# Loads of the first latent head and of the convolutions' gates, issued from ScalarE's queue instead of SyncE's

## The chip, the cores and the metric

One core of a Trainium2 chip runs the whole program in one launch. The metric is device time in microseconds (us), from repeated runs of the same program; the median counts. The engines are TensorE (PE, matrix products; PEld is its loading of weights), VectorE (DVE), ScalarE (ACT), GpSimd (POOL) and SyncE (SP). SP does no arithmetic here: it issues transfers between the chip's large memory (HBM) and the on-chip memory. ACT can issue transfers too. An engine takes its instructions strictly in order, a transfer's issue among them: an instruction that waits holds up all that stand behind it on that engine.

## What is computed

Two layers of a trunk over 1152 tokens (1024 latent, 128 context), width 1024, all in 32-bit floating point. Each layer mixes tokens in four groups of heads that share one input projection, and then applies an MLP:

```python
mq, ckv, kpe, sq, sk, sv, gqkv, gz, ga, gb, hu = project(h, P['w_in'])
o_a = dense_attention(q_a, k, v, MLA_QK ** -0.5, None)     # 4 latent-attention heads
o_b = banded_attention(q_b, k_b, v_b, k_c, v_c, P['swa_sink'])
o_c, _, _ = gdn_mixer(gqkv, gz, ga, gb, P, st[:, 0], st[:, 1])   # delta-net scan
o_d = hyena_mixer(hu, P)                                   # long convolutions
...
z = x1 * long_conv_centred(v, filt[0], P['hy_bias'][0])    # inside hyena_mixer
return x2 * long_conv_centred(z, filt[1], P['hy_bias'][1])
...
x = x + gt1 * rms_norm(merge_heads(o_a, o_b, o_c, o_d), P['g_post_mix'])
x = x + gt2 * rms_norm(square(relu(h @ mlp_w1)) @ mlp_w2, P['g_post_mlp'])
```

The factors x1 and x2 are the gating values of the convolutions. Each layer also needs a modulation vector, a product of the conditioning vector with a weight `w_ada` of 1024 x 6144.

## The kernel before, in words

The program is one long list of instructions made by Python generators; a planner (`TileContext(nc, schedule_with_timeline_sim=True)`) decides at compile time, by its own simulated times, in which order each engine gets them and which buffer each tile takes, and adds the waits. Two generators may therefore end up interleaved on an engine, but what is written first has precedence.

Per layer the input projection runs first and parks its results in HBM (`kscr`, `krscr`, `qscr`, `qrscr`, `vascr` for the latent heads, `uscr` for the three parts v, x1, x2 of the convolutions, `gscr`, `sscr`, `suscr`, `goscr` for the scan). Then three things run side by side, started by `run_timed` at the end of the first half of `layer`: the convolutions (`hyena`, two calls of `long_conv`) followed by attention; the delta-net scan (`gdn_scan`, with precedence by `high_priority`); and the modulation products (`ada`), which stream 256 KB pieces of `w_ada` (tiles `wada`, four buffers in tag T, more in L for the very first) through PE.

`hyena` loads v, the transform matrices and small things, and calls `long_conv` for o = 0 and o = 1. After each it loads x1 or x2 in two halves of 128 x 1024 numbers (512 KB each) with `load(1 + o, i, "x")` and multiplies on DVE (line 1734). The first latent head's `mla_prep` is started from inside the second convolution through `ahead`: its first step issues 16 loads, for Q and K (each a main and a rest part, put together from pieces of 64, 32 and 1 rows), V and one more tile E, and the steps after that compute the scores S on PE and their row maxima on DVE (line 772). Then the negated maxima go by way of HBM (`mscr`) into row 96 of Q, and `mla_main` computes the transposed scores (tile ST), their exponentials on ACT and the weighted sums.

Q, K and V of heads 0, 1 and 3 and all work tiles of the convolutions come from the same pool of 12 buffers (`self.big`), so a load of head 0 has to wait until the convolution is done with a buffer. Head 2 uses the scan's pool.

In the scan each step has a chain of small operations: products on PE (tiles u, dS), an addition on DVE (line 1370), the state's decay on ACT (line 1357), scaled copies on ACT (line 1388) with additions on DVE (line 1389), and stores into `goscr` issued by SP (line 1392). Loads of `wada` are line 392, loads of x and v line 1706, those of head 0 lines 752 to 760. Every transfer of the kernel before is issued by SP.

Of the kernel before, what the change touches and what calls it, by code (L numbers as in the profile page):

```python
# [10 lines left out]
F32 = mybir.dt.float32  # L11
# [9 lines left out]
T = 1152  # L21
# [142 lines left out]
class Trunk:  # L164
# [576 lines left out]
    def mla_prep(self, l, h):  # L741

        nc = self.nc
        tag = self.gdn_tag if h == 2 else self.big
        Q = [self.W(dt=F32R, name="Q", tag=tag) for _ in range(2)]
        K = [self.W(dt=F32R, name="K", tag=tag) for _ in range(2)]
        V = self.W((9, 128), F32R, name="VA", tag=tag)
        E = self.H((128,), F32R, name="vE")
        hp, hr = h // 2, slice(64 * (h % 2), 64 * (h % 2) + 64)
        for i in range(2):  # L750
            for dst, n, r in ((slice(0, 64), self.kscr[l, hp, i], hr), (slice(64, 96), self.krscr[l, i], slice(0, 32))):
                nc.sync.dma_start(out=K[i][dst].bitcast(F32), in_=n[r, 0:T])
                nc.sync.dma_start(out=Q[i][dst, 1024:T].bitcast(F32), in_=n[r, T:1280])
            nc.sync.dma_start(out=Q[i][:64, 0:1024].bitcast(F32), in_=self.qscr[l, hp, i, hr, 0:1024])
            nc.sync.dma_start(out=Q[i][64:96, 0:1024].bitcast(F32), in_=self.qrscr[l, i, 32 * h:32 * h + 32, 0:1024])
            if i == 0:
                nc.sync.dma_start(out=K[0][96:97].bitcast(F32), in_=self.krow[:, 0:T])
                nc.sync.dma_start(out=Q[0][96:97, 1024:T].bitcast(F32), in_=self.krow[:, 0:128])
        nc.sync.dma_start(out=V.bitcast(F32), in_=self.vascr[l, h, 0:9].rearrange("m p c -> p m c"))
        nc.sync.dma_start(out=E.bitcast(F32), in_=self.vascr[l, h, 9])  # L760
        self.job[h] = (Q, K, V, E)
        mx = self.S((8, 3), "mx", 2)
        yield
        for t in range(8):
            q = Q[0][:96, t * 128:t * 128 + 128]
            for a in range(3):
                n = 384 if a < 2 else 512
                ps = self.P(name="S", tag="S" if h else "P")
                self.mm(ps[:, :384], q, K[0][:96, 384 * a:384 * a + 384])
                if a == 2:  # L770
                    self.mm(ps[:, 384:], q, Q[0][:96, 1024:T])
                nc.vector.tensor_reduce(out=mx[:, t, a:a + 1], in_=ps[:, :n], axis=AX.X, op=ALU.max)
                yield
        yield
        yield
        m = self.S((8,), "nm", 2, F32R)
        self.neg_max(m, mx)
        self.row_out(l, h, m.bitcast(F32), 8)
        self.row = nc.sync.dma_start(out=Q[0][96:97, 0:1024].bitcast(F32), in_=self.mscr[l, h:h + 1, 0:1024])
        yield  # L780
# [919 lines left out]
    def hyena(self, l, oT, ahead):  # L1700

        nc = self.nc

        def load(g, i, name):
            t = self.W((4, 256), name=name, tag=self.big)
            nc.sync.dma_start(out=t, in_=self.uscr[l, g, 4 * i:4 * i + 4].rearrange("m p c -> p m c"))
            return t
        fwd = self.dft_mats("fwd", self.small)
        cur = [load(0, i, "v") for i in range(2)]
        inv = self.dft_mats("inv", self.other)  # L1710
        hp = self.W((2, 512), name="hp", tag=self.big)
        for r in (slice(0, 96), slice(96, 97)):
            nc.sync.dma_start(out=hp[r], in_=self.hpscr[l, r])
        up = self.W((3, 256), name="up", tag=self.big)
        nc.sync.dma_start(out=up, in_=self.uscr[l, :, 8].rearrange("g p c -> p g c"))
        up = [up[:, g] for g in range(3)]
        z = up[0]
        fi = self.H(name="fwdp")
        fwdp, invp = (fi[:, a:b].rearrange("p (c f) -> p c f", c=2) for a, b in ((0, 194), (194, 450)))
        nc.sync.dma_start(out=fwdp, in_=self.I["fwdp"])  # L1720
        nc.sync.dma_start(out=invp, in_=self.I["invp"])
        yield HY
        for o in range(2):
            conv = self.long_conv(l, o, cur, fwd, inv, ahead)
            for i, t in enumerate(conv):
                if i == 1:
                    po = self.prompt_conv(l, o, z, hp, fwdp, invp)
                    z = self.H((256,), name="pz")
                    nc.vector.tensor_tensor(out=z, in0=po, in1=up[1 + o], op=ALU.mult)
                yield t  # L1730
            y = self.res
            for i in range(2):
                x = load(1 + o, i, "x")
                nc.vector.tensor_tensor(out=y[i], in0=y[i], in1=x, op=ALU.mult)
            cur = y
        for _ in range(24):
            ahead()
        for c in range(2):
            q = slice(128 * c, 128 * c + 128)
            for m0, src in ((0, cur[0]), (4, cur[1]), (8, z.unsqueeze(1))):  # L1740
                mn = 4 if m0 < 8 else 1
                pt = self.P((4, 128), name="hoT", tag="P")
                for j in range(mn):
                    self.tr(pt[:, j], src[:, j, q])
                oT(6 + c, pt[:, :mn].rearrange("p m t -> p (m t)"), slice(m0 * 128, (m0 + mn) * 128))
            yield HY
# [502 lines left out]
```

## Time and profile before

| | |
|---|---|
| median of 3 runs | 3819.6 us (3818.95 to 3856.05) |
| the profiled execution | 3818.92 us |
| its span, first to last instruction | 3817.1 us |
| PE busy | 3530.3 us, 92% of the span |
| weight loads of PE | 2940.8 us, 77% |
| DVE busy | 2236.0 us, 59% |
| ACT busy | 1367.0 us, 36% |
| POOL busy | 710.1 us, 19% |
| mean granted clock of TensorE | 0.952 of full speed |
| data moved by all transfers | 405.40 MB, mean 106 GB/s |

The busy times are those of one profiled execution and of the whole span; PE's weight loads overlap its products. Issuing a transfer does not count as busy time. Busy shares of the whole span say little about a single stretch, so the rows below are taken from the stretches in which the moved loads are issued.

### The profile page before, as it was taken

Reading aid. Unit: us, or ns where it says so; the run is one execution under the profiler, and the core shown is the slowest. Engines: PE = TensorE matmul, PEld = TensorE weight load, DVE = VectorE, ACT = ScalarE, POOL = GpSimd, SP = SyncE. Lnnn points to the kernel's source line nnn. Section 1 sums busy time; section 2 is a strip of 40 time slices with the busy share of each in tenths; the row PEclk is TensorE's granted clock in tenths of the full one; section 3 lists DMA queues with packets and bytes.
Section 4 is the critical chain, followed back from the end, with each engine's and each line's share of the span. In section 5 each row is a group of like instructions: output and inputs, shape, how many; then the busy total and the mean of one; then the engine's idle time right before and its main releaser. Section 6 shows DMA issues by size and latency. Waiting matters only on the chain. (4 is left out here: it accounts for less than half of the span.)

```text
span 3817.1 us, 58820 instructions
## 1 busy us (share of the span) xinstructions
PE 3530.3 (92%) x22478; PEld 2940.8 (77%) x22478; DVE 2236.0 (59%) x4583; ACT 1367.0 (36%) x2972; POOL 710.1 (19%) x710
## 2 busy tenths in 40 slices
PE   7989888799899999999989798787989999999998
PEld 4879774366689999999968787545656899999997
DVE  5765567677645444444586674767774544444446
ACT  5434343265543122212364334323664422222112
POOL 1152531013420000000131633211143200000003
PEclk9998889799999999999999898897989999999999
DMA  5346476832421111111334465755414211111113
GB/s 203 115 115 158 137 266 201 240 84 60 141 86 48 42 45 44 35 44 45 100 104 129 112 151 151 262 185 167 101 40 138 72 45 45 45 45 45 39 39 122
DMA packets 364677, 405.40 MB, mean 106 GB/s; under 512 B 115816, under 2 KB 237158, under 8 KB 364395
## 3 DMA queue, kind: packets, MB, share of 16 engines
q1 hardware_dynamic: 364394, 401.63, 35.1%
q8 instruction: 177, 2.90, 0.3%
q14 instruction: 106, 0.86, 0.1%
HBM read 298.34 MB, written 103.19 MB: 105 GB/s over the span
## 5 line engine op out<-in xcount | busy, mean ns | idle before, releaser
L213 PE MATMUL hid<-hT,w1h 128*128 128x384 f32 x3072 | 786.6, 335 | 0.1
L213 PE MATMUL pj<-hT,wah 128*128 128x384 f32 x2112 | 575.8, 351 | 10.4 <-ACT wah L253 4.2
L1839 DVE TENSOR_TENSOR acc<-acc,mo 128x512 f32<-128x512 f32 x504 | 345.9, 686 | 391.9 <-PE mo L213 391.9
L213 PEld LDWEIGHTS hid<-hT,w1h 128*128 128x128 f32 x3072 | 557.6, 188 | 14.4 <-ACT h L481 1.1
L213 PE MATMUL hid<-hT,w1l 128*128 128x384 f32 x1536 | 514.1, 335 | 0.0
L213 PE MATMUL mo<-w2h,ul 128*128 128x512 f32 x1116 | 435.0, 392 | 0.0
L213 PE MATMUL mo<-w2h,uh 128*128 128x512 f32 x1080 | 422.7, 391 | 0.0
L213 PE MATMUL mo<-w2l,uh 128*128 128x512 f32 x1080 | 422.7, 391 | 0.0
L213 PEld LDWEIGHTS pj<-hT,wah 128*128 128x128 f32 x2112 | 396.3, 196 | 23.3 <-issue 7.5
L213 PE MATMUL pj<-hT,wal 128*128 128x384 f32 x1056 | 368.2, 349 | 0.7 <-DVE wal L232 0.7
L242 ACT CAST w2h<-w 128x512 fp32r<-128x512 f32 x128 | 70.3, 619 | 732.7 <-PE mo L213 728.5
L269 POOL TENSOR_TENSOR postr<-postr,mhalf 128x1 f32<-128x1 f32 x36 | 22.3, 622 | 1564.1 <-DVE postr L268 1563.7
L213 PEld LDWEIGHTS hid<-hT,w1l 128*128 128x128 f32 x1536 | 288.3, 188 | 2.5
L213 PEld LDWEIGHTS mo<-w2h,ul 128*128 128x128 f32 x1116 | 209.6, 188 | 46.1
L662 POOL TENSOR_TENSOR e<-e,e 128x512 f32<-128x512 f32 (+1 forms) x120 | 162.2, 1353 | 445.3 <-ACT e L651 267.4
L213 PEld LDWEIGHTS mo<-w2h,uh 128*128 128x128 f32 x1080 | 202.8, 188 | 37.5
L213 PEld LDWEIGHTS mo<-w2l,uh 128*128 128x128 f32 x1080 | 202.7, 188 | 36.5
L232 DVE TENSOR_TENSOR el<-e,eh 128x512 fp32r<-128x512 f32 (+1 forms) x252 | 202.3, 820 | 32.2 <-ACT eh L653 30.3
L213 PEld LDWEIGHTS pj<-hT,wal 128*128 128x128 f32 x1056 | 206.4, 195 | 4.6 <-issue 2.0
L1822 DVE SCALAR_TENSOR_TENSOR relu<-hid,relu 128x384 f32<-128x384 f32 x180 | 99.4, 553 | 167.2 <-ACT relu L1821 167.2
L213 PE MATMUL ada<-wada,cst 128*32 128x512 f32 x384 | 137.0, 688 | 46.9 <-DMA wada<-in_w_ada 46.7
L1821 ACT ACTIVATE relu<-hid 128x384 f32<-128x384 f32 x180 | 87.8, 488 | 184.8 <-PE hid L213 184.8
(502 smaller groups left out, 6318.1 us busy)
## 6 DMA issues: line engine op xcount, KB each, us to landing
w<-in_w SPq DMA_DIRECT2D x256, 256.0 KB
wada<-in_w_ada SPq DMA_DIRECT2D x192, 256.0 KB
wa<-in_wa SPq DMA_DIRECT2D x88, 256.0 KB
x<-xres SPq DMA_DIRECT2D x21, 512.0 KB
x<-in_x SPq DMA_DIRECT2D x18, 512.0 KB
Q<-rscr SPq DMA_DIRECT2D x32, 288.0 KB
o<-oscr SPq DMA_DIRECT2D x18, 512.0 KB
xres<-x SPq DMA_DIRECT2D x36, 256.0 KB
```

The source lines that it names most:

```text
L213: self.last = self.nc.tensor.matmul(out, l, r, start=start, stop=stop, skip_group_check=True)
L232: self.nc.vector.tensor_tensor(out=lo, in0=x, in1=hi.bitcast(F32), op=ALU.subtract)
L242: self.nc.scalar.copy(out=hi[:, q], in_=st)
L269: self.nc.gpsimd.tensor_tensor(out=out, in0=out, in1=self.bcs(self.mhalf[:out.shape[0]], out.shape), op=ALU.pow)
L662: self.nc.gpsimd.tensor_tensor(out=acc, in0=acc, in1=e, op=ALU.add)
L1821: nc.scalar.activation(out=r[:, :n], in_=ps[:, :n], func=AF.Relu)
L1822: nc.vector.scalar_tensor_tensor(out=r[:, :n], in0=ps[:, :n], scalar=0.0, in1=r[:, :n], op0=ALU.max, op1=ALU.mult)
L1839: nc.vector.tensor_tensor(out=acc[t][:, ns], in0=acc[t][:, ns], in1=ps, op=ALU.add)
```

## The change

In `mla_prep` a local name `queue` is SP for heads 1 to 3 and ACT for head 0, and all 16 loads of the step are issued on it. In `hyena` the loads of x1 and x2 (g = 1 and 2) are issued by ACT, those of v (g = 0) still by SP. That is 20 issues per layer, 40 in all; bytes, tiles, buffers and arithmetic stay the same. The later load of row 96 of Q (line 779) stays on SP.

```diff
@@ def mla_prep(self, l, h):
         nc = self.nc
+        queue = nc.sync if h else nc.scalar
         tag = self.gdn_tag if h == 2 else self.big
...
-                nc.sync.dma_start(out=K[i][dst].bitcast(F32), in_=n[r, 0:T])
-                nc.sync.dma_start(out=Q[i][dst, 1024:T].bitcast(F32), in_=n[r, T:1280])
-            nc.sync.dma_start(out=Q[i][:64, 0:1024].bitcast(F32), in_=self.qscr[l, hp, i, hr, 0:1024])
-            nc.sync.dma_start(out=Q[i][64:96, 0:1024].bitcast(F32), in_=self.qrscr[l, i, 32 * h:32 * h + 32, 0:1024])
+                queue.dma_start(out=K[i][dst].bitcast(F32), in_=n[r, 0:T])
+                queue.dma_start(out=Q[i][dst, 1024:T].bitcast(F32), in_=n[r, T:1280])
+            queue.dma_start(out=Q[i][:64, 0:1024].bitcast(F32), in_=self.qscr[l, hp, i, hr, 0:1024])
+            queue.dma_start(out=Q[i][64:96, 0:1024].bitcast(F32), in_=self.qrscr[l, i, 32 * h:32 * h + 32, 0:1024])
             if i == 0:
-                nc.sync.dma_start(out=K[0][96:97].bitcast(F32), in_=self.krow[:, 0:T])
-                nc.sync.dma_start(out=Q[0][96:97, 1024:T].bitcast(F32), in_=self.krow[:, 0:128])
-        nc.sync.dma_start(out=V.bitcast(F32), in_=self.vascr[l, h, 0:9].rearrange("m p c -> p m c"))
-        nc.sync.dma_start(out=E.bitcast(F32), in_=self.vascr[l, h, 9])
+                queue.dma_start(out=K[0][96:97].bitcast(F32), in_=self.krow[:, 0:T])
+                queue.dma_start(out=Q[0][96:97, 1024:T].bitcast(F32), in_=self.krow[:, 0:128])
+        queue.dma_start(out=V.bitcast(F32), in_=self.vascr[l, h, 0:9].rearrange("m p c -> p m c"))
+        queue.dma_start(out=E.bitcast(F32), in_=self.vascr[l, h, 9])
@@ def hyena(self, l, oT, ahead): load(g, i, name)
-            nc.sync.dma_start(out=t, in_=self.uscr[l, g, 4 * i:4 * i + 4].rearrange("m p c -> p m c"))
+            (nc.scalar if g == 2 or g == 1 else nc.sync).dma_start(out=t, in_=self.uscr[l, g, 4 * i:4 * i + 4].rearrange("m p c -> p m c"))
```

## Rows read from the trace of the kernel before

**Rows 1.** Stretches; busy us (count) of PE, PEld, DVE, ACT, POOL; clock, DMA share, GB/s.
```profile
600.00:745.00 145.00, 115.77 (x906) 63.08 (x905) 103.42 (x308) 42.90 (x130) 19.62 (x19) 0.85 0.81 238
...
1100.00:1900.00 800.00, 798.77 (x4061) 725.02 (x4061) 398.03 (x655) 189.03 (x382) 26.36 (x25) 1.00 0.16 50
...
2505.00:2650.00 145.00, 109.02 (x719) 63.80 (x718) 104.43 (x279) 37.95 (x102) 23.56 (x22) 0.82 0.64 193
```
**Rows 2.** Who waited for loads (us, times, longest): x, whole run; wada, two stretches.
```profile
  DVE y L1734: 6.7, 3
...
PE ada L213 <- DMA wada<-in_w_ada: 14.8, 11, 4.2
...
PE ada L213 <- DMA wada<-in_w_ada: 30.8, 8, 14.6
```
**Rows 3.** DMA queue of the page: packets, MB, share of 16 engines.
```profile
q1 hardware_dynamic: 364394, 401.63, 35.1%
```
**Rows 4.** Issues on SP, whole run: ns min/median/max, first and last start.
```profile
L753 SPq DMA_DIRECT2D Q<-krscr x16: 308/419/437, 656.1 to 2665.4; - x16
...
L752 SPq DMA_DIRECT2D K<-krscr x16: 317/582/1250, 655.5 to 2664.7; - x16
...
L1706 SPq DMA_DIRECT2D x<-uscr x8: 378/404/499, 604.9 to 2591.8; - x8
```
**Rows 5.** Timeline of SP, layer 2: start us, length us, operation.
```profile
2555.19 0.43 SPq L760 DMA_DIRECT2D vE<-vascr  x1
...
2568.75 0.45 SPq L753 DMA_DIRECT2D Q<-kscr  x1
...
2573.20 0.42 SPq L759 DMA_DIRECT2D VA<-vascr  x1
2573.67 4.68 SPq L392 DMA_DIRECT2D wada<-in_w_ada  x4
```
**Rows 6.** Timeline of PE, layer 2; in brackets the idle time before and its end.
```profile
2565.60 1.06 PE L213 MATMUL ada<-wada,cst 128*32 128x512 f32 x8
...
2582.17 4.00 PE L213 MATMUL ada<-wada,cst 128*32 128x512 f32 x8 [14.60 <-DMA wada<-in_w_ada]
2593.82 3.78 PE L213 MATMUL ada<-wada,cst 128*32 128x512 f32 x8 [7.65 <-DMA wada<-in_w_ada]
```
**Rows 7.** Waits of SP's queue, 2553 to 2575: us, times, longest.
```profile
SPq L1392 <- DVE sc L1389: 8.0, 2, 7.7
```
**Rows 8.** Timeline of SP, layer 1.
```profile
653.77 0.42 SPq L760 DMA_DIRECT2D vE<-vascr  x1
...
666.59 0.43 SPq L759 DMA_DIRECT2D VA<-vascr  x1
...
668.54 1.85 SPq L392 DMA_DIRECT2D wada<-in_w_ada  x4
...
675.54 4.18 SPq L392 DMA_DIRECT2D wada<-in_w_ada  x4
679.81 0.38 SPq L1706 DMA_DIRECT2D x<-uscr  x1
```
**Rows 9.** Timelines of PE and DVE, layer 1.
```profile
673.60 1.92 PE L213 MATMUL ada<-wada,cst 128*32 128x512 f32 x2 [3.43 <-DMA wada<-in_w_ada]
...
687.18 1.23 DVE L1734 TENSOR_TENSOR y<-y,x 128x1024 f32<-128x1024 f32 x1 [2.47 <-DMA x<-uscr]
...
691.93 9.24 DVE L772 TENSOR_REDUCE mx<-S 128x1 f32<-128x384 f32 x18
```
**Rows 10.** First convolution step; main attention's score products by layer: first to last start.
```profile
L1461 DVE TENSOR_TENSOR pm<-v,v x2: 691/692/692, 546.3 to 2437.0; 128x512 f32<-128x512 f32 x2
...
L213 PEld LDWEIGHTS ST<-Q,K x228: 186/190/193, 728.7 to 912.1; 96*128 96x128 f32 x76, 97*128 97x128 f32 x38
...
L213 PEld LDWEIGHTS ST<-Q,K x228: 186/190/338, 2629.0 to 2793.4; 96*128 96x128 f32 x76, 97*128 97x128 f32 x38
```

## The prediction

> **What bounds the kernel now.** I first cut the run into stretches [rows 1]. The MLP stretch keeps the matrix engine (PE) busy 798.77 of 800 us at full clock with the DMA engines 0.16 busy: no load is late there, and nothing that the change touches can shorten it. The loads that it moves are issued in the two stretches where the long convolutions, the delta-net scan and the start of attention overlap, 600 to 745 in layer 1 and 2505 to 2650 in layer 2. There PE is busy 115.77 and 109.02 of 145 us, the clock falls to 0.85 and 0.82, and the DMA engines are 0.81 and 0.64 busy, while ACT works only 42.90 and 37.95. So these stretches are chains of short steps beside heavy loading, and PE idles 29 + 36 = 65 us in them: whatever the change brings must come out of that, and it is 1.7% of the span.
>
> Next I asked who waits for the moved loads. For x, the product at line 1734 on DVE waited three times, 6.7 us in all [rows 2]. For Q, K, V and E of head 0 nothing waited at all. What does wait is PE, in order, for the modulation weights (wada): 14.8 us in 530 to 740 and 30.8 us in 2430 to 2640 [rows 2]. Those weights leave on SP, as every load does now: one hardware queue carries 401.63 MB [rows 3]. So the loads of head 0 matter, if at all, through what stands behind them in SP's queue.
>
> **The change part by part.** *Removed from SP.* Sixteen loads of head 0 and four of x in each layer. One issue of the K and Q pieces holds SP for 0.419 to 0.582 us at the median, one of x for 0.404 [rows 4]. I take 0.5 for each of the sixteen (the two one-row loads are shorter, so this is a little high): 8.0, and 4 x 0.404 = 1.6, so 9.6 per layer and 19.2 us in all. SP's time is worth nothing by itself; what counts is what is queued past it.
>
> In layer 2 PE finishes eight modulation matmuls at 2565.60 + 1.06 = 2566.7 and has used up the weights it had; the next four loads leave only at 2573.67, and PE stands for 14.60 us until 2582.17 [rows 5, 6]. In between SP first waits for the scan: 7.7 of the 8.0 us on line 1392 [rows 7], which the change leaves alone, and then, from 2568.75 to 2573.20 + 0.42, six remaining loads of head 0 with a few others between them: 6 x 0.47 (their median prices) makes **2.8 us** by which the weights can leave earlier. In layer 1 the head's loads begin at 653.77, the last (VA) at 666.59, the weights leave at 668.54 and PE waits 3.43 us until 673.60 [rows 8, 9]; four of the head's loads stand directly ahead, 4 x 0.47: **1.9 us**. Bounds: nothing (the bytes still pass through the same DMA engines), and the whole of the three PE waits, 14.60 + 7.65 + 3.43 = 25.7 us [rows 6, 9], if the weights no longer queue behind the head's bytes at all. I stay near the lower end since the rows price the issue only. This is hidden no further: when PE is released, the modulation matmuls, then the scores of head 0, follow directly.
>
> *x.* The third layer-1 load of o = 1 leaves at 679.81 behind four wada issues begun at 675.54, and DVE stands 2.47 us before its product at 687.18 [rows 8, 9]; the other two waits of the 6.7 are in layer 2. On ACT's queue these loads stand behind nothing of SP. Bounds 0 and 6.7; I take the whole **6.7**, because behind that product DVE goes on to the maxima of head 0's scores, eighteen of them in one stretch of 9.24 us from 691.93 on [rows 9], with no idle time that could swallow the wait.
>
> The Trainium skill ("DMA: Bandwidth & Descriptors", section "Issuing engines are not separate DMA queues") speaks against this term: transfers from any engine run on the same 16 DMA engines and interleave, and a second issuer saves only the time to initiate. By it the x term would be near nil; the sum without it is given as a rival below. No run here shows a load on another queue.
>
> *Added to ACT.* The same 40 issues, 19.2 us if an issue costs there what it costs on SP; no row shows one on ACT. Bounds: 0, and all 19.2 on the path. ACT is busy 80.85 of 290 us, 28% [rows 1], so in most of the idle time an issue hides behind nothing that ACT has to do. But the scan's steps on ACT (the decays at line 1357, the scaled products at 1388) are short and on a chain with PE and DVE, and an issue ahead of one delays it. With the 28% as the chance that one is due, 0.28 x 19.2 = **5.4 us** on the path.
>
> *New waits on ACT.* A load of head 0 waits for a free buffer of the 12 that the convolution uses, or for an earlier transfer. SP now spreads them over 653.77 to 667.02 and 2555.19 to 2573.62 [rows 5, 8], 31.7 us, of which 16.0 are the issues: 15.7 us of waiting and other work. If the compile-time order puts a load on ACT where its buffer is free, that costs nothing; if ACT reaches it early, all scan and convolution steps behind it on ACT wait, and the PE and DVE steps that follow them. I take 0 and keep 15.7 for the range.
>
> *Order.* The planner writes the order of all engines from its own simulated times, so everything after about 600 us may be shuffled. The two layers show what order and company can do to one piece of work: from the first convolution step to the first main attention matmul it takes 728.7 - 546.3 = 182.4 us in layer 1 and 2629.0 - 2437.0 = 192.0 in layer 2 [rows 10]. So I keep 9.6 us per layer, of either sign, for the range, and 0 for the sum.
>
> **Sum:** 2.8 + 1.9 + 6.7 - 5.4 = 6.0 us gained. The profiled execution took 3818.9 us (span 3817.1 and 1.8 around it), which makes 3812.9; the median of the runs is 0.7 above it. I say **3813 us**.
>
> **Rivals.** *A, the queue bypass.* If two queues are served in turn, the wada loads no longer wait behind the 2.4 MB of head 0 (from its tiles' shapes), nor x behind wada. Then most of the 25.7 us of PE waits and the 6.7 of x go: with half of the first, 12.9 + 6.7 less ACT's 5.4 is 14 us, 3805; with all of it 27, so 3792. For it: PE's 14.60 us idle is far longer than the 2.8 of issues. Against: the DMA engines are 0.64 to 0.81 busy, and what PE gains early it then waits for in the scores, since K and Q land later. The skill's same page (section "Queues, rings and completion order") says that a DMA engine goes round the queue rows that have work, a packet at a time; that is this rival's mechanism, and no row before the change can show it.
>
> *B, issue time only.* The transfers interleave and only SP's issue time is saved: 4.7 against ACT's 5.4, no change, 3819.
>
> *C, ACT is held up.* Loads at the head of ACT's queue wait for buffers of the convolution or earlier transfers, and the scan and convolution steps wait behind them. Price: ACT's issues 19.2 and the 15.7 of waiting, less the gain of 11.4, so up to 23 us slower, 3842; with half the waits and half the issues, 17.5 less 11.4, 3825. It decides once the waits on ACT are over 6.0 us in all, 0.2 us for each of the 32 head loads. For it: ACT reaches such a load earlier than SP, which is kept busy by wada. Against: in layer 1 SP got through all sixteen in 13.25 us, 8.0 of them issues [rows 8], so the buffers came free about as fast as the loads could leave.
>
> *D, the order is shuffled for the worse or better*, by up to 19 us over both layers, 3800 to 3838, and beyond that where the attention stretches are reordered too.
>
> **How the numbers follow.** Forecast 0.35, A 0.25, B 0.15, C 0.17, D 0.08. No single one of them leaves 1% (38 us, about what a measurement of this kernel can tell from no change); only A with all its waits plus a kind order, or C with an unkind one, does. Faster by over 1% 0.06, within 0.87, slower by over 1% 0.07. Range: down to A with all waits and some of D, 3788; up to C in full, 3842.
>
> **What would show it.** Forty issues on ACT's queue in the changed profile, 0.4 to 0.6 us each, and idle time of DVE before line 1734 for x gone: then the x term holds. The wada loads in layer 2 leaving about 3 us sooner after PE's eighth matmul, and PE's 14.60 us wait shorter by that: then the SP term; shorter by 8 or more, rival A. ACT steps of lines 1357 and 1388 starting later after their input is ready, with a DMA issue ahead of them: the ACT term, and if the issue itself stood waiting, C. The first main attention matmul, 728.7 and 2629.0 now, should come 2 to 4 us earlier in each layer, and the MLP stretches should keep their length. I am wrong if the first main matmul moves by more than 10 us in either layer, or if the time is lost or won outside these two stretches.

## The result, and the profile after

The changed kernel took 3849.9 us (median of 17 executions, 3831.6 to 3869.8), the kernel before 3821.9 (17, 3805.8 to 3856.1): 1.0066 times as long, 95% interval 1.0042 to 1.0090. I had said 3813 and a range up to 3842. The sign was wrong and the time is outside the range. It is within the 1% either way to which I had given 0.87; but 17 executions of each tell 0.24% apart, and not only the 1% that I had taken for the least.

The page of the changed kernel: the line of the span, that of busy time, the row of the granted clock, and from the list of DMA queues the two hardware queues.

```profile
span 3843.8 us, 58831 instructions
...
PE 3553.5 (92%) x22478; PEld 2956.9 (77%) x22478; DVE 2228.9 (58%) x4583; ACT 1366.5 (36%) x2972; POOL 716.4 (19%) x710
...
PEclk9999899799999999999999898888969999999999
...
q1 hardware_dynamic: 356002, 392.58, 34.0%
q10 hardware_dynamic: 8392, 9.06, 0.8%
```

The loads did move: 9.06 MB leave on a second queue. The engines execute as many instructions as before, and PE is busy for 23.2 us longer (its weight loads for 16.1, POOL for 6.3; DVE for 7.1 less). Time that appears as longer matmuls, not as waits, points at the clock, and one slice of the clock row reads 6.

The two stretches of [rows 1] in which the moved loads are issued, changed kernel (start and end, length, then busy us and instructions of PE, PEld, DVE, ACT and POOL, granted clock, DMA share, GB/s):

```profile
600.00:745.00 145.00, 110.14 (x840) 59.02 (x842) 101.49 (x293) 39.06 (x119) 19.56 (x19) 0.87 0.76 229
2505.00:2650.00 145.00, 115.44 (x879) 70.69 (x877) 107.55 (x293) 49.54 (x133) 26.09 (x22) 0.85 0.62 185
```

The clock is no lower here than before (0.87 and 0.85 against 0.85 and 0.82). But stretches of fixed times hold different work in two programs: 840 matmuls against 906 in the first, 879 against 719 in the second. So I cut layer 2 by its own events instead: first convolution step, first main attention matmul, first output projection, first MLP matmul. Each row is one of these three stages. The kernel before:

```profile
2437.00:2629.00 192.00, 143.12 (x1085) 81.06 (x1085) 139.76 (x402) 44.28 (x144) 36.13 (x37) 0.84 0.73 230
2629.00:2885.30 256.30, 239.87 (x1475) 160.82 (x1476) 188.18 (x330) 160.59 (x315) 81.31 (x60) 0.94 0.27 67
2885.30:3001.60 116.30, 110.93 (x513) 87.14 (x512) 48.53 (x103) 51.57 (x109) 29.68 (x32) 1.00 0.41 134
```

The changed kernel, with layer 1's first two stages above:

```profile
542.00:728.60 186.60, 144.68 (x1202) 80.24 (x1202) 136.24 (x410) 49.79 (x168) 34.45 (x36) 0.87 0.74 237
728.60:1009.30 280.70, 263.11 (x1542) 165.00 (x1541) 195.97 (x347) 160.84 (x316) 79.23 (x59) 0.95 0.35 91
...
2443.40:2614.50 171.10, 132.50 (x1068) 77.55 (x1068) 124.67 (x379) 43.03 (x145) 35.68 (x36) 0.83 0.73 230
2614.50:2900.70 286.20, 273.02 (x1508) 184.40 (x1508) 196.18 (x350) 160.82 (x315) 80.56 (x59) 0.84 0.28 68
2900.70:3028.20 127.50, 116.74 (x512) 91.24 (x512) 49.47 (x103) 52.01 (x109) 32.14 (x33) 0.95 0.37 122
```

Layer 2's convolutions end 20.9 us sooner, which looks like a large success; attention then takes 29.9 us longer and the output projection 11.2. So the loss isn't where the loads are issued, but behind it. Layer 1 begins its convolutions 4.3 us sooner (542.0 against 546.3) and is 4.2 us longer in its first stage and 4.3 in its second (276.4 before), and both MLPs keep their length. In layer 2's attention the clock is 0.84 against 0.94. In the output projection PE's idle time doubles (127.5 - 116.74 = 10.8 us against 5.4).

The waits that the prediction was about are almost gone. Layer 2's PE waits for wada from 2437 to 2660, changed kernel, beside the 30.8 us of [rows 2]:

```profile
PE ada L213 <- DMA wada<-in_w_ada: 4.6, 7, 2.1
```

DVE's wait for x, 6.7 us before, has no row any more. If one stopped here, one would say that the second queue worked and something else undid the gain. Both halves of that had to be tested.

Why suspect the order: when the two compiled programs are laid side by side, instruction by instruction, the planner has given 3148 of layer 2's PE instructions another place, and 332 of layer 1's. In PE's order in layer 2, for example, 16 score matmuls for row maxima (S) now stand in one run just after head 0's main attention; before, they were spread among other work.

### The profile page after: what moved, and what is told of

Same layout as the page of the kernel before. It is cut to its first block, busy times and chain, and to the rows that moved or that the text cites. A ratio compares the mean times of both kernels' runs of the same rounds, so it can differ in the third digit from the quotient of the medians.

```text
span 3843.8 us, 58831 instructions
## 1 busy us (share of the span) xinstructions
PE 3553.5 (92%) x22478; PEld 2956.9 (77%) x22478; DVE 2228.9 (58%) x4583; ACT 1366.5 (36%) x2972; POOL 716.4 (19%) x710
## 3 DMA queue, kind: packets, MB, share of 16 engines
q10 hardware_dynamic: 8392, 9.06, 0.8%
## 5 line engine op out<-in xcount | busy, mean ns | idle before, releaser
L213 PEld LDWEIGHTS mo<-w2h,uh 128*128 128x128 f32 x1080 | 202.8, 188 | 37.5
L232 DVE TENSOR_TENSOR wal<-wa,wah 128x512 fp32r<-128x512 f32 x88 | 63.3, 724 | 175.2 <-ACT wah L253 127.8
L1822 ACT ACTIVATE relu<-hid 128x384 f32<-128x384 f32 x180 | 87.8, 488 | 184.5 <-PE hid L213 184.5
```

The costliest lines, as they stand in the source:

```text
L213: self.last = self.nc.tensor.matmul(out, l, r, start=start, stop=stop, skip_group_check=True)
L232: self.nc.vector.tensor_tensor(out=lo, in0=x, in1=hi.bitcast(F32), op=ALU.subtract)
L1822: nc.scalar.activation(out=r[:, :n], in_=ps[:, :n], func=AF.Relu)
```

## The experiments

Theory: the move itself is worth about nothing, and the loss is the order that the planner wrote anew. Rivals: the loads on ACT cost the time themselves (queue); or the two kernels differ only by how the clock happened to fall.

The tool for it: build the program once as one kernel to learn each engine's order, then build it again as the other, with every instruction chained behind its predecessor in that order by a dependency that costs no semaphore. Loads that change their engine are left out of the chain. Order and queue can then be crossed. In short:

```
order = order_of(trace(arrays, head=ORDER, gate=ORDER))      # where the order comes from
nc = trace(arrays, order, head=QUEUE, gate=QUEUE)            # where the 40 loads leave
...
for e, names in order.items():
    for a, b in zip(names, names[1:]):
        tc.add_manual_dep(here[b], a, no_sync, reason="order")
```

**e1: old order, loads on ACT** (ORDER before, QUEUE after).

> All 40 loads leave from ScalarE's queue as in the changed kernel, but every engine keeps the instruction order of the kernel before (the other instructions are chained in that order, engine by engine; only the 40 loads are placed anew). Theory 'order': the move itself gains a little or nothing, and the loss comes from the order that the planner wrote anew; so the time is 0.996 to 1.002 of before, layer 2's attention keeps its 256 us (first main attention matmul to first output projection), and its out-projection stretch 116 us. Rival 'queue': the issues on ScalarE or the loads' new company cost the time themselves; then this is as slow as the changed kernel, 1.004 to 1.009, although the order is the old one. Rival 'clock by chance': the two kernels differ only by how often the clock falls in a run; then this lies anywhere from 0.998 to 1.008 and its profile shows the fall at other places.

**e2: new order, loads on SP** (ORDER after, QUEUE before).

> The counterpart: all loads leave from SP's queue as before, but every engine keeps the instruction order of the changed kernel. Theory 'order': as slow as the changed kernel or slower, 1.004 to 1.011, with layer 2's attention near 286 us, half of the clock in a piece of it, and VectorE waiting again for x. Rival 'queue': back to 1.000 (0.998 to 1.002). Rival 'clock by chance': anywhere from 0.998 to 1.008.

Measured: e1 1.0025 (0.9998 to 1.0051), e2 1.0089 (1.0053 to 1.0124). With all loads back on SP and only the order kept, the loss is all there, so the loads on ACT are not needed for it. Both programs have the order that they were to have: PE's operations come in the recorded sequence, but for starts that lie too close together to tell. Layer 2's attention and output projection in e1:

```profile
2648.70:2904.60 255.90, 238.94 (x1475) 160.36 (x1476) 189.03 (x330) 160.75 (x315) 81.32 (x60) 0.95 0.27 67
2904.60:3022.70 118.10, 112.92 (x513) 88.69 (x511) 48.19 (x103) 51.38 (x109) 29.47 (x31) 0.98 0.40 132
```

and in e2:

```profile
2626.00:2920.70 294.70, 280.03 (x1509) 187.24 (x1509) 196.23 (x350) 160.69 (x315) 79.95 (x59) 0.82 0.27 66
2920.70:3047.10 126.40, 117.06 (x512) 91.53 (x512) 48.84 (x103) 51.88 (x109) 31.35 (x33) 0.95 0.37 123
```

The stage lengths go with the order, not with the queue. So do the waits. The wait rows of PE for wada and of DVE for x (layer 1, then layer 2), in e1:

```profile
PE ada L214 <- DMA wada<-in_w_ada: 28.3, 7, 14.2
...
DVE y L1736 <- DMA x<-uscr: 4.6, 2, 4.3
...
DVE y L1736 <- DMA x<-uscr: 2.4, 2, 1.6
```

and in e2:

```profile
PE ada L214 <- DMA wada<-in_w_ada: 8.7, 3, 5.8
```

Of the 26.2 us by which PE's waits for wada in layer 2 shrank (30.8 to 4.6), 22.1 are gone with SP as the only queue too (30.8 to 8.7). The wait for x is 7.0 us on ACT's queue in the old order, and nil on SP's in the new one, where I had expected DVE to wait again. One more thing was not as the theory had it: e1 is at 1.0025, above the 1.002 that I had given it. A small loss is left, though its interval just holds 1. No run had everything as before with the chain alone; e10 and e11 below come nearest, with the old order, SP and a changed end of layer 2, at 1.0019.

**e3 and e4: parts of the change**, the planner free.

```
e3:  load():     nc.sync.dma_start(...)          # gate loads back on SP
e4:  mla_prep(): queue = nc.sync                 # head 0's loads back on SP
```

> Only the 32 loads of head 0 leave from ScalarE's queue; the gate loads of the convolutions stay on SP; the planner orders freely. Theory 'order': the planner shuffles again, in another way, so the ratio is not a share of the whole change's 1.0066; it lies from 0.995 to 1.010, and it moves by where layer 2's attention finds a low clock. Rival 'queue': the head's loads are most of what moved (32 of 40), so 1.004 to 1.008.

> Only the gate loads (x, two of the three operands in each layer) leave from ScalarE's queue; head 0's loads stay on SP; the planner orders freely. Theory 'order': another shuffle, from 0.995 to 1.010, whatever the number of loads. Rival 'queue': 8 loads of 0.4 us each can cost at most 3 us, so 0.998 to 1.001, and e3 and e4 together add up to the whole change's 1.0066.

Measured: e3 1.0049 (1.0026 to 1.0072), e4 1.0072 (1.0045 to 1.0098). Eight loads cost as much as forty; the parts add up to 1.0121 and not to 1.0066. That speaks against every price per load. For 'order' it is a weak test, since 0.995 to 1.010 could hardly be missed. e4 also warns: its profiled execution has a span of 3826.3 us, and its median is 3852.5.

**e5 and e6: which layer's order**, loads on ACT, the order taken from one kernel for layer 1 and from the other for layer 2.

> All 40 loads leave from ScalarE's queue; layer 1's instructions keep the changed kernel's order, layer 2's the order of the kernel before. Theory 'layer-2 order' (nearly all of the reordering lies in layer 2: 3148 of its matrix-engine instructions stand elsewhere, 332 of layer 1's): close to before, 0.999 to 1.003; layer 2 from its first convolution step to its MLP about 565 us. Rival 'layer-1 order': as slow as the changed kernel, 1.005 to 1.009.

> The counterpart: all 40 loads from ScalarE's queue, layer 1 in the old order, layer 2 in the changed kernel's. Theory 'layer-2 order': 1.004 to 1.009, with the out-projection stretch of layer 2 at 125 to 128 us (116 before) and its attention slow. Rival 'layer-1 order': 0.999 to 1.003.

Measured: e5 1.0026 (0.9995 to 1.0057), e6 1.0034 (1.0004 to 1.0063). The difference has the expected sign but is small, and the intervals overlap; e6 fell short of its 1.004. By the times alone this pair doesn't decide. The stages go with layer 2's order: e6 has the output projection of 127.2 us and an attention of 282.4 at 0.87, e5 has 116.7 and 257.8 at 0.94, and its layer 2 takes 566.4 us from the first convolution step to the MLP, as expected. With e1 this makes two runs at 1.0025 and 1.0026 that have layer 2's old order and the loads on ACT. So a small cost of the move itself isn't excluded; no stage of these two profiles shows where it would lie.

**e7: one load**, V of head 0 in layer 1.

```
-        nc.sync.dma_start(out=V.bitcast(F32), ...
+        (nc.scalar if h == 0 and l == 0 else nc.sync).dma_start(out=V.bitcast(F32), ...
```

> A single load moved: V of head 0 in layer 1 leaves from ScalarE's queue, the other 39 stay on SP. The planner writes layer 2 anew all the same (3151 matrix-engine instructions of layer 2 stand elsewhere than before, close to the changed kernel's order; 170 of layer 1's). Theory 'layer-2 order': as slow as the whole change, 1.004 to 1.009, from one load in the other layer. Rival 'queue': one issue of about 0.5 us moved can't be seen, 0.999 to 1.001.

**e8: layer 2's loads alone.**

```
mla_prep(): queue = nc.scalar if h == 0 and l else nc.sync
load():     (nc.scalar if g and l else nc.sync).dma_start(...)
```

> Only layer 2's 20 loads leave from ScalarE's queue; layer 1 keeps queue and order, and the planner orders layer 2 freely, this time near the order of the kernel before up to the end of the convolutions. Theory 'layer-2 order': without the changed kernel's early part of layer 2 the loss stays away: 0.997 to 1.003, and the gain of the move in layer 2 that was forecast (2.8 us of issue, about 4 of x, less 2.7) may show as 0.998 to 1.000. Rival 'queue': half of the whole loss, 1.003.

Measured: e7 1.0014 (0.9986 to 1.0043), e8 1.0076 (1.0047 to 1.0106). Both forecasts missed, and the misses were the most useful of the runs. One moved load rewrote layer 2, but not to the whole loss; half of the loads, with an order that is near the old one up to the end of the convolutions, gave all of it. The rows of attention and output projection in e7:

```profile
2611.60:2905.80 294.20, 274.87 (x1508) 184.86 (x1509) 199.91 (x351) 161.40 (x317) 79.82 (x60) 0.84 0.26 67
2905.80:3022.90 117.10, 111.86 (x514) 88.11 (x512) 48.53 (x103) 50.44 (x107) 29.70 (x32) 0.99 0.40 133
```

and in e8:

```profile
2615.50:2898.10 282.60, 265.75 (x1498) 177.93 (x1498) 194.85 (x346) 161.94 (x315) 81.34 (x59) 0.87 0.25 63
2898.10:3025.90 127.80, 116.22 (x512) 90.90 (x512) 49.18 (x103) 51.95 (x109) 31.77 (x33) 0.95 0.37 122
```

e7 has the slow attention without the slow output projection. So these are two separate pieces, and in all kernels so far the ratio is over 1.003 where the output projection takes 124 us or more (changed, e2, e3, e4, e6, e8) and 1.0026 or less where it takes 116 to 118 (e1, e5, e7). e8 has both pieces, and its convolutions, at 183.7 us, gain less than the 20.9 us that pay for a part of the loss in the changed kernel.

*What happens in the output projection.* From there on the new order differs from the old one in a handful of places only. SP's timeline in the changed kernel (start, length, operation):

```profile
2922.43 3.80 SPq L1799 DMA_DIRECT2D x<-xres  x7
2926.84 0.37 SPq L1769 DMA_DIRECT2D o<-oscr  x1
2928.12 4.90 SPq L241 DMA_DIRECT2D w<-in_w  x2
2933.12 0.86 SPq L1804 DMA_DIRECT2D xres<-x  x2
2934.86 0.37 SPq L1769 DMA_DIRECT2D o<-oscr  x1
```

and the same loads in the kernel before:

```profile
2901.86 1.38 SPq L1798 DMA_DIRECT2D x<-xres  x3
2903.67 0.37 SPq L1768 DMA_DIRECT2D o<-oscr  x1
2904.10 4.34 SPq L1798 DMA_DIRECT2D x<-xres  x4
```

The o load that the next group of tokens needs stood after three loads of the residual and now stands after seven. Behind it the weight loads hold SP for 4.90 us (0.87 before), and a second o load leaves only at 2934.86. Who pays, changed kernel, ACT and then PE:

```profile
2937.73 1.04 ACT L1771 CAST oh<-o 128x1024 fp32r<-128x1024 f32 x1 [2.80 <-DMA o<-oscr]
...
2938.83 0.79 PE L213 MATMUL op<-woh,oh 128*128 128x512 f32 x1 [4.00 <-ACT oh L1771]
```

PE's 4.00 us are followed by a piece at half clock: the matmuls there start 0.43 us apart (2939.42, 2939.85); before the wait they start 0.23 apart.

**e9: the changed kernel with the old sequence in layer 2's output projection and MLP; e10: the reverse; e11: the reverse for SP alone.**

```
def with_tail(order, other, engines):     # in short; instructions from 27700 on: output projection and MLP of layer 2
    for e in engines:
        new = iter([n for n in other[e] if num(n) >= 27700])
        order[e] = [next(new) if num(n) >= 27700 else n for n in order[e]]

e9:  with_tail(after, before, all),  loads on ACT
e10: with_tail(before, after, all),  loads on SP
e11: with_tail(before, after, SP),   loads on SP
```

> The changed kernel with its own order, except that in layer 2's output projection and MLP each engine keeps the sequence of the kernel before: five instructions move (one load of an o tile on SP, its cast to oh, one squared sum and two weight casts on ScalarE, with one product of VectorE and one weight load on SP beside them). Theory 'two pieces' (about half of the loss is the output projection of layer 2, which stands for o loads queued late; the other half is a clock that falls at new places in layer 2's attention): the out-projection stretch goes from 127.5 to 116 to 118 us and the ratio from 1.0066 to 1.003 to 1.005. Rival 'clock only': the stretch stays near 127 or what it gains is lost elsewhere; 1.006 to 1.008.

> The counterpart: the kernel before, all loads on SP, with the changed kernel's sequence in layer 2's output projection and MLP alone. Theory 'two pieces': the stretch goes from 116 to 125 to 128 us and the ratio to 1.002 to 1.004. Rival 'clock only': 116 us, 1.000.

> As e10, but only SP's sequence is the changed one (one o load behind four more loads of the residual, one weight load ahead of a small one); ScalarE and VectorE keep the old sequence. If the late o load on SP is the cause: 1.002 to 1.004 and the stretch near 125 us, as in e10. If the cast to oh that ScalarE has behind other work is the cause: 1.000 and near 117.

Measured: e9 1.0020 (0.9995 to 1.0045), e10 1.0019 (0.9994 to 1.0045), e11 1.0019 (0.9995 to 1.0042). The stretch, in e9 and then in e10:

```profile
2910.10:3031.00 120.90, 114.27 (x513) 89.35 (x513) 49.20 (x103) 51.94 (x109) 31.66 (x33) 0.97 0.39 129
```

```profile
2902.00:3026.10 124.10, 113.14 (x514) 89.10 (x513) 48.32 (x103) 51.84 (x109) 29.57 (x32) 0.97 0.38 126
```

Undone, the stretch shrinks by 6.6 us, and not by the 9.5 and more that I had expected; done alone, it grows by 7.8, and by 4.6 with SP's part only (120.9 in e11, where I had expected 125). PE's wait for oh there is 6.0 us in e10 and 3.9 in e11, against 0.2 in the kernel before. So SP's sequence makes over half of it by itself, and the rest comes with the later sequence of ACT and DVE, the cast to oh in it, and with a clock at half for 6.8 us in e10 and 3.4 in e11. That e9 gained 0.46% in all, 18 us where the stretch gave 6.6, and came out below the 1.003 expected, is more than this mechanism explains; the intervals are wide enough to hold it. And e10, with 124.1 us and 1.0019, breaks the rule by output projection above. By their times, neither piece alone can be told from no loss (attention: e7, e9; output projection: e10, e11).

*The two pieces over all profiles.* In the five profiles with layer 2's old order (before, e1, e5, e10, e11) its attention takes 255.9 to 257.8 us, in the nine with a new one (changed, e2 to e4, e6 to e9, and e12 below) 270.7 to 295.7. Together with the convolutions, which the new order shortens, that is 449.1 us on average in the five and 459.9 in the nine: 10.8 us lost. The output projection takes 116.3 to 120.9 us in the five profiles in which its own sequence is the old one (before, e1, e5, e7, e9) and 124.1 to 127.8 in the eight with the changed one (all others but e11), 117.8 and 126.4 on average: 8.6 us lost. Together that is 19.4 of the 22 us, in two nearly equal pieces.

*What happens in attention.* The changed kernel in steps of 5 us, around two of the places where its clock falls:

```profile
2645.00:2650.00 5.00, 4.76 (x32) 2.84 (x31) 3.36 (x7) 0.52 (x1) 0.00 (x0) 1.00 0.00 0
2650.00:2655.00 5.00, 4.22 (x11) 2.06 (x10) 4.55 (x9) 0.00 (x0) 0.00 (x0) 0.69 0.00 2
...
2785.00:2790.00 5.00, 5.00 (x32) 2.66 (x31) 2.60 (x7) 0.08 (x1) 0.00 (x0) 1.00 0.00 0
2790.00:2795.00 5.00, 3.99 (x15) 2.76 (x15) 3.48 (x13) 0.75 (x3) 0.00 (x0) 0.68 0.01 3
2795.00:2800.00 5.00, 5.00 (x13) 2.97 (x12) 3.07 (x4) 3.18 (x6) 2.92 (x3) 0.50 0.10 29
...
2845.00:2850.00 5.00, 5.00 (x23) 3.45 (x15) 4.21 (x10) 3.15 (x8) 2.69 (x3) 0.51 0.00 0
2850.00:2855.00 5.00, 5.00 (x46) 3.88 (x46) 3.62 (x6) 2.83 (x11) 2.54 (x3) 1.00 0.18 39
```

Both places are runs of score matmuls for row maxima, where PE stops several times, for 0.2 to 0.6 us, for DVE's maxima (from PE's timeline):

```profile
2649.27 0.44 PE L213 MATMUL S<-K,Q 96*128 96x384 f32 x1 [0.24 <-DVE mx L773]
...
2650.55 0.90 PE L213 MATMUL S<-K,Q 96*128 96x384 f32 x2 [0.38 <-DVE mx L773]
...
2791.05 0.38 PE L213 MATMUL sS<-sK,sQ 64*128 64x256 f32 x1 [0.62 <-DVE smx L928]
```

At the second of these, the third in time, the clock then stays at half, 1.2 GHz, for 58.0 us, though PE is busy throughout. In the profiles of all kernels that have layer 2's new order (changed, e2, e3, e4, e6 to e9) the clock falls at 37 to 41, 133 to 136 and 176 to 191 us after layer 2's first main matmul; in none of those with the old one (before, e1, e5, e10, e11) does it fall between 20 and 190 us.

**e12: the sparse places filled**: the changed kernel in its own order, with these score matmuls issued three times over (in short).

```
def mmk(self, key, out, l, r):
    self.mm(out, l, r)
    for _ in range(2 * (key in DUP)):
        self.mm(out, l, r)
```

> The changed kernel in its own order, with 25 of the score matmuls for row maxima (S and sS) of layer 2 issued three times over into the same tile, at the three places in layer 2's attention where the clock fell (36, 131 and 175 us after its first matmul). 50 more matmuls of 0.16 to 0.2 us, 8 to 10 us of work that partly fills gaps in which the matrix engine waits for VectorE's maxima. Theory 'sparse maxima': the clock falls there because the engine has little to do per time; with the gaps filled it does not fall at 36, 131 and 175 us, mean clock back near 0.947, ratio 1.002 to 1.007. Rival 'clock by something else': the falls stay at these places and the ratio goes to 1.007 to 1.009.

Measured: 1.0055 (1.0035 to 1.0075). At the first place, which is 2655 to 2665 here (the three places are 37, 133 and 177 us behind the first main matmul by the rows of the clock):

```profile
2655.00:2660.00 5.00, 5.00 (x36) 3.71 (x28) 2.75 (x6) 0.00 (x0) 0.00 (x0) 1.00 0.00 0
2660.00:2665.00 5.00, 4.86 (x23) 3.38 (x22) 4.09 (x7) 0.00 (x0) 0.00 (x0) 1.00 0.01 2
```

The first fall is gone in this one profile, and all eight profiles of a new order without the extra matmuls have it. The other two stayed, for 6.8 and 37.5 us. So "sparse maxima" is borne out at the first place only, and what makes the clock fall at the other two stays open. The mean clock over e12's executions is 0.9463, against 0.9438 for the changed kernel. By the 29 us for each 0.010 below, that would be worth about 7 us, and the extra matmuls were priced at 8 to 10: the time is within the error of the changed kernel's.

*How much of the loss is clock.* Each execution has its time and mean granted clock. Over the 30 executions of the kernel before that ran beside e1 to e4, a fitted line falls by 29 us for each 0.010 of clock. Their mean is 0.9477, the changed kernel's 17 have 0.9438: 0.0039 makes 11 us, half of the 22 us between the two means (3828.8 and 3851.0; the 17 executions of the kernel before that ran beside the changed kernel have a mean of 3827.0 and no clock on record). The rest, 11 us at equal clock, is as long as what the output projection grew by (11.2), a part of which is clock again; the shorter convolutions and layer 1 go into it too, so I take the agreement for rough.

No version beat the kernel before. The nearest is e7, 1.0014.

## Why the prediction was wrong, point by point

**The step that failed** is *Order*: "0 for the sum", with 9.6 us per layer of either sign kept for the range. With all loads back on SP and only the order kept (e2) the kernel is at 1.0089, so the order suffices for the whole loss. I priced it from how one stretch varied between the two layers (182.4 and 192.0 us, [rows 10]), and only up to the first main matmul. The stretch did move, by 20.9 us in layer 2, over twice that bound; and the loss came after it, in attention and output projection, which no term of the sum touched. Rival D had the mechanism, "beyond that where the attention stretches are reordered too", with a chance of 0.08.

**SP's issue time**, 2.8 us in layer 2: the size is near, the path was another, so that is luck. In the old order PE waits 28.3 (e1) and 27.6 us (e5) for wada there with the loads on ACT, and 30.8, 30.6 (e10) and 33.6 (e11) with them on SP. But the weights did not leave 3 us sooner behind PE's eighth matmul. SP and then PE in e1:

```profile
2592.83 3.12 SPq L393 DMA_DIRECT2D wada<-in_w_ada  x4
```

```profile
2584.87 1.06 PE L214 MATMUL ada<-wada,cst 128*32 128x512 f32 x8
2601.02 4.91 PE L214 MATMUL ada<-wada,cst 128*32 128x512 f32 x8 [14.18 <-DMA wada<-in_w_ada]
2611.66 4.09 PE L214 MATMUL ada<-wada,cst 128*32 128x512 f32 x8 [5.73 <-DMA wada<-in_w_ada]
```

They leave 2592.83 - 2585.93 = 6.9 us behind it, and 7.0 in the kernel before [rows 5, 6]. SP is rid of the head's loads there and waits longer for other things, among them 2.5 us (0.2 before) for stores into goscr to land before it loads them back. So the wait of 14.60 us shrank by 0.4 only; the next one, 7.65 [rows 6], shrank by 1.9. In layer 1, where I had 1.9, the total of both layers and the start of the run fell only from 46.7 to 44.0, so 0.2 is left.

**x, 6.7 us**: not shown as a gain of the queue. In the old order with the loads on ACT the waits are 7.0 in e1, but 2.2 in e6 (layer 1) and 0.2 in e5 (layer 2). They changed their cause: on SP the load stood behind wada [rows 8]; in e1 the last x load of layer 1 (the second of o = 1, which the prediction calls the third) leaves ACT at 681.19, just after a scan step that had kept ACT waiting 5.53 us for PE. In the changed kernel's order the waits vanish with either queue (changed, e2).

**ACT's issues, 5.4 us lost**: not shown either. In e1 the stretch from the first convolution step to the first main matmul is 182.7 and 191.0 us, against 182.4 and 192.0. All local terms together gained 0.7 us where I had 6.0, and in e11, with all loads on SP, the same stretches are 184.5 and 195.9, so 0.7 is within what one profile differs from the next. The forty issues take 0.23 to 0.68 us each on ACT in the changed kernel, much as on SP.

**Waits on ACT, 0**: right as far as the stretches show, and rival C's 6 to 23 us are not there. In the changed kernel one scan step waits 1.0 us for a K load. Before line 1422 in layer 1 the trace puts 9.3 us of ACT's idle time down to an x load; ACT waited 13.1 us at this place before, for POOL.

**Rival A**, the bypass: its sign was there, PE's waits for wada in layer 2 went from 30.8 to 4.6, but by the order; between e2 and the changed kernel the queue's share is 8.7 - 4.6 = 4.1 us, and with the order held the wait of 14.60 us kept 14.18. **Rival B**, issue time only, no change, comes nearest to what the move is worth once the order is held. The Trainium skill ("DMA: Bandwidth & Descriptors", section "Issuing engines are not separate DMA queues"), set against the x term in the prediction, says that a second issuer saves only the time to initiate. e1 agrees, with 7.0 us of waits for x against 6.7 and 1.0025 (0.9998 to 1.0051) in all.

**What would show me wrong** did: the first main matmul of layer 2 moved by 14.5 us (2629.0 to 2614.5), and the time was lost outside the two stretches. The MLPs kept their length, as said.

## What to carry to other kernels

Where a planner writes the order, an edit has two prices, its own and that of the new order; compare the two orders before pricing the edit, and cross order and queue to measure them apart, since here one moved load put 3151 of layer 2's matrix-engine instructions elsewhere, and eight cost as much as forty. A stage that ends 20 us sooner has gained nothing until the next stages are added: follow it to the end of the layer. One profile isn't the kernel where the clock wanders: e4's profiled span and its median differ by 26 us.

## What I had not expected of the hardware

The granted clock can stay at half while PE is busy 5.00 of every 5 us, here for 58.0 us (2795 to 2850 above lie in it). The Trainium skill ("TensorE: Matmul & The Clock Gate", section "Seeing it yourself") says that the clock events of a trace can't be fully trusted and tells of a clock stuck at a quarter for over 50 us. Here the start distances bear such rows out: in the long fall two 128x512 products of O start 0.43 us apart (2801.18, 2801.61), and at full clock, at 2647.82 and 2648.05, 0.23.

In layer 2's attention the clock falls where the order puts it, but for how long is chance: the fall 176 to 191 us into it took 58.0 us in the changed kernel and 10.2 in e4. In layer 1's attention whether it falls is chance too. e10 keeps order and queue of the kernel before all through layer 1. Both have this stage, and 10 us of it, here, the kernel before first:

```profile
728.70:1005.10 276.40, 261.11 (x1544) 165.64 (x1544) 197.83 (x350) 161.52 (x317) 79.34 (x60) 0.96 0.35 91
910.00:920.00 10.00, 9.39 (x46) 5.86 (x45) 7.98 (x18) 6.60 (x15) 4.25 (x3) 1.00 0.17 48
```

```profile
728.00:1025.30 297.30, 282.57 (x1545) 179.20 (x1545) 196.65 (x350) 161.50 (x317) 78.24 (x59) 0.88 0.33 84
910.00:920.00 10.00, 10.00 (x24) 6.18 (x24) 4.62 (x12) 3.87 (x9) 3.81 (x3) 0.50 0.17 47
```

The fall in e10 begins 182 us into the stage and lasts 51.2 us; e1 and e11 have it too (47.8 and 44.4 us), and the profile of the kernel before doesn't. A difference of this size, 20.9 us between two profiles of the same instructions, is no evidence on an edit.
